# A decoder layer on one core: 128 attention weights a query instead of 256, the farthest keys in pass 1 and pass 3, two buffers for pass 3's loads

## The chip, the cores and the metric

One Trainium2 core of one chip. The metric is device time in microseconds of one execution of the kernel; "before" is the median of 3 runs.

## What is computed

One layer for 2048 tokens of width 1024, in float32. The part that the change touches is the dilated attention: 8 heads of 64, three branches whose results are merged by their softmax denominators.

```python
DILATIONS = ((128, 1), (512, 4), (2048, 16))
...
q = _rope(_rmsnorm(q.reshape(B, S, N_HEADS, HEAD_DIM), q_norm[i]), positions)
k = _rope(_rmsnorm(k.reshape(B, S, N_HEADS, HEAD_DIM), k_norm[i]), positions)
...
kk = jnp.concatenate([k_prev, kb], axis=2)
scores = jnp.einsum('nbqhd,nbkhd->nbhqk', qs, kk).astype(jnp.float32) * (HEAD_DIM ** -0.5)
dist = (jnp.arange(BLK)[:, None] + BLK) - jnp.arange(2 * BLK)[None, :]
band = (dist >= 0) & (dist <= n_back)
...
w = jax.nn.softmax(jnp.stack(lses, axis=0), axis=0)
o = jnp.sum(w[..., None] * jnp.stack(outs, axis=0).astype(jnp.float32), axis=0)
```

Within a residue class a query at place p of its block of 128 sees the keys p to 127 of the block before and the keys 0 to p of its own: 129 keys, of which only place p counts twice. In the third branch there is no block before. Around the attention stand RMSNorm and one input projection to seven groups of 512 columns (q, k, v, gate_B, u, v_A, gate_A), a gMLP mixer per chunk of 128 tokens, an output projection, and a gated per-layer embedding.

## The kernel before, in words

The work runs in three passes over 16 tiles of 128 tokens. Every float32 product is made of three float32r (or float16) products of a high and a low part, so one projection of a tile to 512 columns is 24 matmuls.

**Pass 1** (functions `prep`, `step`, `post_qk`, `turn_qk`, `post_v`, `post_gb`). `prep(n)` normalises tile n of x (L213, L150, L151, L219), turns it with two DMA transposes of 16-bit words (`turn_words`: L182 on ACT, L184 on SP, L186 on DVE) and splits it to `aT` (L196 on ACT, L197 on DVE). `step(n, g)` projects a tile to q, k, v or gate_B. What follows a q or k projection is norm and rotary on DVE and POOL (L411 to L429), a DMA transpose (L438), for k a copy on ACT (L444), and a store to DRAM. The scheduler of the framework sets each engine's order. At the end TensorE's order is written by hand: q of tiles 14 and 15 back to back, then both k, both v, both gates, then the first gMLP chunk, whose weights are loaded by `load_group` (L130 to L138) into the slots of q, k and v as these come free.

**Pass 2** (class `Step`, function `gmlp`). Every head pair and branch has 16 query tiles, in quads of four. A step makes the scores of one tile whose keys are two blocks wide (27 of a head pair's 48 tiles, 108 in all), or of two tiles with one block (first blocks, and all of the third branch): 152 steps. `scores` (L780) fills a PSUM bank, DVE adds the mask and takes the row minimum (L783, L789), ACT makes the weights (L791) in `pr`. `turn`, one step later (LAG_B), splits the 512 weights per query row into two float16 parts (L798 on ACT, L117 on POOL) and turns them by one DMA transpose (L801) from `raw` into `pt`. `values`, six steps after the scores (LAG_C), multiplies with v (L812). Between `turn` and `values` `fill(1.3)` puts 1.3 us of gMLP matmuls (L651, yields of two matmuls for 0.43 us) into TensorE's order.

**Pass 3** (`mixed`, `merge`, `turn_mixed`, `out_proj`, `norm3`, `gate`). `mixed(n)` loads the three branches (`ob`, L602, L604), gate and gMLP output (`ma`, `mg`), `merge` weighs and adds them (L573 to L590). `out_proj` and `gate` are 108 matmuls a tile (L230). Between the passes the last three gMLP chunks run beside the loads of the output weights.

Of the kernel before, what the change touches and what calls it, by code (L numbers as in the profile page):

```python
# [10 lines left out]
F32 = mybir.dt.float32  # L11
F32R = mybir.dt.float32r
F16 = mybir.dt.float16
I32 = mybir.dt.int32
U16 = mybir.dt.uint16
# [21 lines left out]
def _shape_constants():  # L37

    p = np.arange(128)

    def mask(keys, back=False):
        keep = keys[None, :] >= p[:, None] if back else keys[None, :] <= p[:, None]
        return np.where(keep, 0, NEG).astype(np.float32)
    k0 = p.reshape(32, 4).T.reshape(128)
    return {"c_ident": np.eye(128, dtype=np.float32),
            "c_mask": np.concatenate([mask(k0, True), mask(k0), mask(p, True), mask(p)], 1),
            "c_freq": INV_FREQ.reshape(1, 32)}
# [3 lines left out]
PR, PH, OB, SV = 3, 6, 5, 5  # L51

LAG_B, LAG_C = 1, 6

BLOCK0, FILL = 18, 1.3
# [26 lines left out]
def hybrid_layer(ctx: ExitStack, tc: tile.TileContext, io, out):  # L82
# [17 lines left out]
    d_gb = dram.tile([S, 512], F32, name="d_gb")  # L100
    d_at = dram.tile([NT, 128, D], F32, name="d_at")
# [5 lines left out]
    cst.tile([128, 8], F32, name="pad")  # L107
    bs = cst.tile([128, 4], F32, name="bs")
# [151 lines left out]

    def load_qk(qk, hp, c):
# [13 lines left out]
    with ExitStack() as s1, ExitStack() as s1q:  # L275
# [90 lines left out]
        def v_scale():  # L366
# [3 lines left out]
            ones = p1.tile([128, 128], F32, name="ones")  # L370
# [37 lines left out]
        def post_qk(n, which, ps):  # L408
# [8 lines left out]
            m1 = p1.tile([128, HEADS, 2, 32], F32, name="m1", bufs=2)  # L417
# [8 lines left out]
            nc.vector.tensor_tensor(r, r, rs[:, :, None].to_broadcast([128, HEADS, 64]), op=OP.mult)  # L426
            hl = p1.tile([128, HEADS, 2, 64], F16, name="hl", bufs=2)
# [26 lines left out]

        def post_v(n, ps):
# [4 lines left out]
            hi = nc.scalar.activation(vt[:, :, 0, 0:64], z, AF.Copy, scale=sv)  # L460
            lo = nc.vector.scalar_tensor_tensor(vt[:, :, 1, 0:64], z, sv, vt[:, :, 0, 0:64],
# [15 lines left out]
        def gm_constants():  # L477
            for name, src in (("mask", io["c_mask"]), ("wsT", d_ws),
                              ("lng", bcast(io["ln_v_g"], 512)), ("lnb", bcast(io["ln_v_b"], 512))):
                CG[name] = pg.tile([128, 512], F32, name=name)  # L480
                nc.sync.dma_start(CG[name], src)

        def spatial_weights():
# [4 lines left out]
            nc.sync.dma_start(keep[:, 0:128], io["c_mask"][:, 384:512])  # L488
# [11 lines left out]
        def step(n, g):  # L500
# [3 lines left out]
            if g in "qk":  # L504
# [3 lines left out]
                turn_qk(n, which, hl)  # L508
            else:
# [59 lines left out]
    def merge(ob, mx):  # L569
        ov = ob.rearrange("p (b q) e -> p b q e", b=3)  # L570
        nm, den = ov[:, :, :, 130:132], ov[:, :, :, 64:130:65]
        mn = small.tile([128, 4, 2], F32, name="mn")
        nc.vector.tensor_reduce(mn, nm.rearrange("p b q h -> p q h b"), axis=AX.X, op=OP.min)  # L573
        w = small.tile([128, 3, 4, 2], F32, name="w", bufs=3)
        nc.vector.tensor_tensor(w, mn[:, None].to_broadcast([128, 3, 4, 2]), nm, op=OP.subtract)
        nc.scalar.activation(w, w, AF.Exp)
        wd = small.tile([128, 3, 4, 2], F32, name="wd", bufs=3)
        nc.vector.tensor_tensor(wd, w, den, op=OP.mult)
# [3 lines left out]
        nc.vector.tensor_tensor(w, w, mn[:, None].to_broadcast([128, 3, 4, 2]), op=OP.mult)  # L582
        nums = ob[:, :, 0:130].rearrange("p b (h d) -> p b h d", h=2)[:, :, :, 0:64]
        wb = w.rearrange("p b q h -> p (b q) h")[:, :, :, None].to_broadcast([128, 12, 2, 64])
        nc.vector.tensor_tensor(nums, nums, wb, op=OP.mult)  # L585
        o = nums[:, 0:4]
        nc.gpsimd.tensor_tensor(o, o, nums[:, 4:8], op=OP.add)  # L587
        nc.gpsimd.tensor_tensor(o, o, nums[:, 8:12], op=OP.add)
        m = mx.rearrange("p (q h d) -> p q h d", q=4, h=2)
# [6 lines left out]
    def mixed(n):  # L596

        rows = slice(n * 128, (n + 1) * 128)
        ob = pm.tile([128, 12 * OW + 16], F32, name="ob")[:, 0:12 * OW].rearrange("p (b e) -> p b e", b=12)
# [29 lines left out]
    with s2:  # L629
        p2 = s2.enter_context(tc.tile_pool(name="p2", bufs=1))  # L630

        lng, lnb, mask = (CG[n] for n in ("lng", "lnb", "mask"))
# [102 lines left out]
        def first(br, j):  # L735
            return j < (1, 4, NT)[br]
# [19 lines left out]

        class Step:
# [220 lines left out]
```

## Time and profile before

| | |
|---|---|
| runs | 1285.12, 1286.45, 1288.18 us (median 1286.45) |
| profiled execution | 1282.93 us, span 1281.2 us, mean granted clock 0.978 |
| busy in the span | PE 1196.0 us (93%), PEld 973.7, DVE 884.9, ACT 648.3, POOL 513.3 |
| pass 1 | 0 to 416 us, to the end of the second long TensorE idle |
| pass 2 | 416 to 817 us, to the last product with v |
| pass 3 and its start | 817 to 1281 us |

PE is TensorE's matmuls, PEld its weight loads, which overlap them; SPq is SyncE's queue, which issues the DMAs. Times in the trace count from the span's start. The profiled execution is 3.5 us under the median of the runs.

### The profile page before, as it was taken

Reading aid. Unit: us, or ns where it says so; the run is one execution under the profiler, and the core shown is the slowest. Engines: PE = TensorE matmul, PEld = TensorE weight load, DVE = VectorE, ACT = ScalarE, POOL = GpSimd, SP = SyncE. Lnnn points to the kernel's source line nnn. Section 1 sums busy time; section 2 is a strip of 40 time slices with the busy share of each in tenths; the row PEclk is TensorE's granted clock in tenths of the full one; section 3 lists DMA queues with packets and bytes.
Section 4 is the critical chain, followed back from the end, with each engine's and each line's share of the span. In section 5 each row is a group of like instructions: output and inputs, shape, how many; then the busy total and the mean of one; then the engine's idle time right before and its main releaser. Section 6 shows DMA issues by size and latency. Waiting matters only on the chain.

```text
span 1281.2 us, 21314 instructions
## 1 busy us (share of the span) xinstructions
PE 1196.0 (93%) x7166; PEld 973.7 (76%) x7166; DVE 884.9 (69%) x2253; ACT 648.3 (51%) x1273; POOL 513.3 (40%) x454
## 2 busy tenths in 40 slices
PE   5899999999596999999899899969999999999998
PEld 4778888888485787777677688758778888888887
DVE  6885556565576688878777778588766766766733
ACT  5754433433345487677687678333334334334422
POOL 4763334343354465566565556332221121221200
PEclk9999999999898999999999999989999999999999
DMA  7499777768669999999999999845546646655431
GB/s 266 142 220 219 157 171 175 171 173 186 149 182 245 237 194 236 226 223 241 225 222 251 237 193 220 233 148 174 154 120 144 183 122 137 163 147 135 138 91 50
DMA packets 440542, 233.80 MB, mean 182 GB/s; under 512 B 337136, under 2 KB 389104, under 8 KB 440432
## 3 DMA queue, kind: packets, MB, share of 16 engines
q1 hardware_dynamic: 440432, 232.44, 76.2%
q8 instruction: 56, 0.92, 0.3%
q14 instruction: 54, 0.44, 0.1%
HBM read 102.99 MB, written 57.54 MB: 125 GB/s over the span
## 4 chain that ended last, share of the span: by engine, by line
PE 53%; DMA 15%; DVE 14%; issue 7%; ACT 6%; POOL 3%; SPq 2%; DVEq 0%; ACTq 0%; POOLq 0%
PE mm L230 21%; PE gt L230 7%; PE s L230 7%; PE mm L651 7%; DMA pt<-raw 6%; PE pt L230 4%; PE av L230 2%; PE s L780 2%; PE pt L812 2%; DVE pr L783 2%; DMA raw<-w_in 1%; DVE aT L197 1%; DVE wslot L138 1%; DMA st<-hl 1%; DMA ob<-d_o 1%
## 5 line engine op out<-in xcount | busy, mean ns | idle before, releaser
L230 PE MATMUL mm<-wslot,aT 128*128 128x512 f32 x1536 | 365.8, 393 | 20.2 <-ACT aT L196 16.2
L230 PEld LDWEIGHTS mm<-wslot,aT 128*128 128x128 f32 x1536 | 290.9, 190 | 83.9 <-ACT aT L196 18.0
L651 PE MATMUL mm<-wslot,aT 128*128 128x512 f32 x1152 | 314.1, 413 | 24.0 <-DVE gv L642 18.5
L651 PEld LDWEIGHTS mm<-wslot,aT 128*128 128x128 f32 x1152 | 211.2, 195 | 64.1 <-DVE gv L642 19.3
L117 POOL TENSOR_TENSOR raw<-pr,raw 128x512 f16<-128x512 f32 (+1 forms) x152 | 177.8, 1175 | 138.6 <-ACT raw L798 124.2
L791 ACT ACTIVATE pr<-pr,ost 128x256 f32<-128x256 f32 (+1 forms) x384 | 150.1, 451 | 69.5 <-DVE ost L789 64.4
L230 PE MATMUL gt<-wslot,aT 128*128 128x512 f32 x600 | 143.8, 392 | 1.0 <-ACT wslot L136 1.0
L230 PEld LDWEIGHTS gt<-wslot,aT 128*128 128x128 f32 x600 | 112.8, 189 | 25.7 <-ACT wslot L136 2.2
L812 PEld LDWEIGHTS <-pt 128*128 128x128 f16 x1800 | 64.7, 98 | 62.3 <-DMA pt<-raw 33.5
L798 ACT ACTIVATE raw<-pr 128x512 f16<-128x512 f32 (+1 forms) x152 | 93.2, 620 | 33.1 <-DMA pt<-raw 30.6
L812 PE MATMUL pt<-sv,pt 128*128 128x65 f16 x1800 | 81.6, 194 | 21.1 <-DMA pt<-raw 19.0
L783 DVE CUSTOM_DVE_ANT_0 pr<-s,mask 128x256 f32<-128x256 f32 (+1 forms) x256 | 81.1, 357 | 18.3 <-POOL raw L117 14.2
L230 PE MATMUL s<-wslot,aT 128*128 128x512 f32 x384 | 91.1, 392 | 0.0
L424 POOL TENSOR_TENSOR m<-m,m 128x512 f32<-128x512 f32 x32 | 49.8, 1557 | 96.7 <-DVE rsh L150 90.3
L230 PEld LDWEIGHTS s<-wslot,aT 128*128 128x128 f32 x384 | 72.8, 190 | 15.2
L230 PE MATMUL pt<-wslot,aT 128*128 128x512 f32 x336 | 78.3, 389 | 0.0
L230 PEld LDWEIGHTS pt<-wslot,aT 128*128 128x128 f32 x336 | 63.1, 188 | 13.1
L780 PEld LDWEIGHTS <-sq 128*128 128x128 f16 x768 | 69.9, 120 | 3.4 <-issue 1.6
L590 POOL TENSOR_TENSOR ma<-ob,ma 128x512 f32<-128x512 f32 x16 | 24.1, 1506 | 120.0 <-DMA ma<-d_gb 61.1
L780 PE MATMUL s<-sk,sq 128*128 128x256 f16 (+1 forms) x512 | 71.9, 276 | 0.0
L587 POOL TENSOR_TENSOR ob<-ob 128x512 f32<-128x512 f32 x16 | 20.9, 1309 | 124.8 <-DVE ob L585 124.8
L789 DVE TENSOR_SCALAR ost<-ost 128x2 f32<-128x2 f32 (+1 forms) x152 | 63.0, 416 | 2.6
(198 smaller groups left out, 1797.4 us busy)
## 6 DMA issues: line engine op xcount, KB each, us to landing
xt<-x SPq DMA_DIRECT2D x32, 512.0 KB, 4.5
d_o<-ost SPq DMA_DIRECT2D x48, 264.0 KB, 3.7
raw<-w_in SPq DMA_DIRECT2D x38, 256.0 KB, 3.3
sv<-d_vt SPq DMA_DIRECT2D x32, 264.0 KB, 3.7
ob<-d_o SPq DMA_DIRECT2D x16, 528.0 KB, 4.5
xt<-d_at SPq DMA_DIRECT2D x16, 512.0 KB, 4.7
sk<-d_k SPq DMA_DIRECT2D x32, 256.0 KB, 4.6
out<-th SPq DMA_DIRECT2D x32, 256.0 KB, 2.8
```

Source lines behind the costliest of these rows:

```text
L117: nc.gpsimd.tensor_tensor(dst, a, b, op=op)
L230: nc.tensor.matmul(ps, aT[:, ha, k, :], w(slot, hw, k), start=(n == 0), stop=(n == 3 * nk - 1))
L424: add = nc.gpsimd.tensor_tensor(f1, f1, f2, op=OP.add)
L587: nc.gpsimd.tensor_tensor(o, o, nums[:, 4:8], op=OP.add)
L590: nc.gpsimd.tensor_tensor(m, o, m, op=OP.mult)
L651: nc.tensor.matmul(ps, GT[c][:, ha, k, :], slots[g][:, hw, k, :], start=(n == 0), stop=(n == 23))
L780: nc.tensor.matmul(ps[:, c:c + nk], cols(br, j, Q[h]), cols(br, j, K, n, h, self.nb), start=(n == 0), stop=(n == 1))
L783: nc.vector.tensor_tensor_reduce(pr[:, c:c + nk], ps[:, c:c + nk], mask[:, m - nk:m], -1.0, 3e38, op0=OP.add, op1=OP.min, accum_out=o[:, j ...
L789: nc.vector.tensor_scalar(nm, nm, math.log(PSCALE), None, op0=OP.add)
L791: nc.scalar.activation(pr[:, c:c + nk], pr[:, c:c + nk], AF.Exp, bias=o[:, j - j0, 130 + h:131 + h], scale=-1.0)
L798: nc.scalar.activation(ph, pr[:, :width], AF.Copy)
L812: nc.tensor.matmul(PO[0][:, j % 2, h], self.pt[:, t, c // 128], vt[:, h, vv, 0:65], start=(n == 0), stop=(n == 3 * self.nb - 1))
```

## The change

**Pass 2.** For a tile with two key blocks the scores of the own block are overwritten, where the key stands after the query, by those of the block before (`copy_predicated` with the mask as predicate). So 128 weights a query stand for 128 of the 129 keys. A step is now always one tile (192 steps); a `Pair` of tiles 2i and 2i+1 shares one `turn` (96 in all). After the transpose `part` takes the two blocks apart again: DVE ands the words with a table of bits into `pc` (own block), POOL subtracts that from `pt` (block before). The weights' matmuls stay as they were. LAG_C is 9 steps, `part` runs 6 steps after the scores, `fill` takes 0.9 us after a one-block tile and 1.13 us after a two-block tile.

**The 129th key** (one or four tiles back, branches 1 and 2). Pass 1 makes its score by `far_scores` on POOL (product) and DVE (sum), 27 of each, and stores it with plain float32 v (`vr`). Pass 3 loads both and merges them as two more branches.

**Pass 3's loads** `ob`, `ma`, `mg` get two buffers. **Pass 1's tail**: tile 14 is prepared before the steps of tile 13, tile 15 between them.

```diff
-        for g in "qkvg":
+        prep(NT - 2)
+        for g in "qk":
             step(NT - 3, g)
-        prep(NT - 2)
         prep(NT - 1)
+        for g in "vg":
+            step(NT - 3, g)
...
+        def far_scores(n):
+            far = small.tile([128, 2, HEADS], F32, name="far", bufs=2)
+            if n < FAR[1]:
+                nc.vector.memset(far, -NEG)
+            for x, back in enumerate(FAR):
+                if n >= back:
+                    t = p1.tile([128, HEADS, 64], F32, name="m2", bufs=2)
+                    f = t.rearrange("p h d -> p (h d)")
+                    pool_tt(f, RT["k", n - back], RT["q"][1], OP.mult)
+                    nc.vector.tensor_reduce(far[:, x], t, axis=AX.X, op=OP.add, negate=True)
+            nc.sync.dma_start(d_far[n], far)
...
+            nc.scalar.activation(vr, ps, AF.Copy, scale=sv)
+            nc.sync.dma_start(d_vr[n * 128:(n + 1) * 128], vr)
...
+            def part(self, br, after):
+                with tc.issue_after(after.ins):
+                    nc.vector.tensor_tensor(d, a, bits[:, None, None, m:m + 64].to_broadcast([128, 2, 2 * n, 64]),
+                                            op=OP.bitwise_and)
+                pool_tt(a, a, d, OP.subtract)
...
+                if nb == 2:
+                    own = ps[:, :, 128:256]
+                    nc.vector.copy_predicated(own, m.bitcast(U32)[:, None].to_broadcast([128, 2, 128]),
+                                              ps[:, :, 0:128])
+                    self.last = nc.vector.tensor_reduce(top, own, axis=AX.X, op=OP.max, negate=True)
...
+                nc.scalar.activation(top, top, AF.Copy, bias=math.log(PSCALE))
+                for h in range(2):
+                    nc.scalar.activation(pr[:, h], own[:, h], AF.Exp, bias=top[:, h:h + 1],
+                                         scale=1.0 if nb == 2 else -1.0)
...
-LAG_B, LAG_C = 1, 6
+LAG_B, LAG_P, LAG_C = 1, 6, 9
-BLOCK0, FILL = 18, 1.3
+BLOCK0, FILL = 18, (0.9, 1.13)
```

In `merge` two columns of weights, a copy, a product `vr * w` (DVE) and two additions (POOL) are added per tile.

ACT in pass 1, one tile's period, before (`hl<-st` is L444, the copy that waits for the transpose of k; `raw<-xt` starts the next tile's transposes):

```order
L470 ACTIVATE gb<-pt 128x512
L213 ACTIVATE aT,ss<-xt 128x1024
L444 ACTIVATE hl<-st 128x1024
L182 ACTIVATE raw<-xt 128x1024 x2
L411 ACTIVATE sq<-mm 128x512
L182 ACTIVATE raw<-raw 128x256 x4
```

and in the change:

```order
L500 ACTIVATE gb<-pt 128x512
L221 ACTIVATE aT,ss<-xt 128x1024
L440 ACTIVATE hl<-kr 128x8x64
L190 ACTIVATE raw<-xt 128x1024 x2
L456 ACTIVATE hl<-st 128x1024
L421 ACTIVATE sq<-mm 128x512
L190 ACTIVATE raw<-raw 128x256 x4
```

The copy `hl<-st` now stands behind `raw<-xt`, and the rounding of k (`hl<-kr`) ahead of it.

POOL in the same period, in the change (L125 are the two products of the 129th key, L434 the rotary additions, L159 the inverse roots; before, L402, L424, L404, L151 followed each other there):

```order
L159 TENSOR_TENSOR rs<-rs,mhalf 128x1
L434 TENSOR_TENSOR m_2229<-m_2229,m_2230 128x512
L159 TENSOR_TENSOR rsh<-rsh,mhalf 128x8
L412 TENSOR_TENSOR ta<-gA,cs 128x128
L125 TENSOR_TENSOR m_2242<-kr,m_2229 128x512
L125 TENSOR_TENSOR m_2245<-kr,m_2229 128x512
L159 TENSOR_TENSOR rsh<-rsh,mhalf 128x8
L434 TENSOR_TENSOR kr<-kr,m_2282 128x512
L414 TENSOR_TENSOR tb<-gB,sn 128x128
```

Both products stand between the rotary addition of q and that of k.

DVE in pass 2, two-block tiles of the second branch, in the change (L870 folds the blocks, L872 is the row maximum, L838 takes a pair apart, L897 moves the product with v):

```order
L870 COPY_PREDICATED s<-mask,s 128x2x128
L872 TENSOR_REDUCE ost<-s 128x2
L838 TENSOR_TENSOR pc<-pt,bits 128x512
L870 COPY_PREDICATED s<-mask,s 128x2x128
L872 TENSOR_REDUCE ost<-s 128x2
L897 COPY ost<-pt 128x2x130
L870 COPY_PREDICATED av<-mask,av 128x2x128
L872 TENSOR_REDUCE ost<-av 128x2
```

Where two tiles had four L783 with their read-outs and two L789, they now have two foldings, two maxima, and one L838 that waits for a transpose in this queue.

## Rows read from the trace of the kernel before

**Rows 1.** The page's chain that ended last, share of the span by engine.

```profile
PE 53%; DMA 15%; DVE 14%; issue 7%; ACT 6%; POOL 3%; SPq 2%; DVEq 0%; ACTq 0%; POOLq 0%
```

**Rows 2.** Busy us by engine in stretches of 50 us; then clock, DMA share, GB/s.

```profile
100.00:150.00 50.00, 50.00 (x222) 41.44 (x221) 28.18 (x56) 20.61 (x35) 19.37 (x18) 1.00 0.84 198
...
850.00:900.00 50.00, 45.40 (x201) 37.02 (x202) 45.04 (x77) 21.48 (x39) 15.35 (x12) 0.93 0.52 166
...
1000.00:1050.00 50.00, 50.00 (x222) 41.39 (x221) 34.83 (x70) 20.06 (x37) 9.62 (x8) 1.00 0.58 161
```

**Rows 3.** TensorE's waits in 350:400, 400:450 and 450:800: us, times, longest.

```profile
PE mm L230 <- ACT aT L196: 13.8, 1, 13.8
...
PE mm L651 <- DVE gv L642: 12.3, 1, 12.3
...
PE pt L812 <- DMA pt<-raw: 15.7, 19, 2.5
```

**Rows 4.** Timeline of TensorE, behind the two long waits of pass 1.

```profile
352.57 8.01 PE L230 MATMUL mm<-wslot,aT 128*128 128x512 f32 x24 [13.75 <-ACT aT L196]
...
416.41 8.49 PE L651 MATMUL mm<-wslot,aT 128*128 128x512 f32 x24 [12.32 <-DVE gv L642]
```

**Rows 5.** Timeline of DVE: the last split of tile 5 and of tile 15.

```profile
119.70 0.69 DVE L197 TENSOR_TENSOR aT<-raw,aT 128x512 fp32r<-128x512 f32 x1
...
355.61 0.68 DVE L197 TENSOR_TENSOR aT<-raw,aT 128x512 fp32r<-128x512 f32 x1
```

**Rows 6.** Timeline of ACT: the copy of k ahead of the next tile's words.

```profile
342.83 1.13 ACT L444 ACTIVATE hl<-st 128x1024 f16<-128x1024 f16 x1 [3.31 <-DMA st<-hl]
```

**Rows 7.** Timeline: an addition on POOL and the small operation of DVE beside it.

```profile
355.84 1.59 POOL L424 TENSOR_TENSOR m<-m,m 128x512 f32<-128x512 f32 x1 [0.49 <-DVE m L421]
356.21 1.24 DVE L150 TENSOR_SCALAR rsh<-ssh 128x8 f32<-128x8 f32 x1
```

**Rows 8.** Groups of instructions, shapes apart: busy us, mean ns, idle before.

```profile
L117 POOL TENSOR_TENSOR gv<-gv,lng 128x512 f32<-128x512 f32 x16 | 20.6, 1289 | 9.5 <-DVE gv L669 6.4 <-ACT raw L798 0.9 <-DVE ost L789 0.8
L428 ACT ACTIVATE hl<-m 128x512 f16<-128x512 f32 x32 | 20.2, 630 | 79.6 <-DVE m L426 79.6
L413 DVE TENSOR_REDUCE ssh<-sq 128x8 f32<-128x512 f32 x32 | 21.8, 680 | 43.4 <-ACT sq L411 43.4
L150 DVE TENSOR_SCALAR rs<-ss 128x1 f32<-128x1 f32 x32 | 4.8, 150 | 12.1 <-ACT aT L213 12.1
```

**Rows 9.** Stretches of pass 2, columns as in rows 2, and their sum.

```profile
417.00:450.00 33.00, 31.09 (x190) 23.87 (x189) 21.15 (x72) 16.51 (x35) 16.40 (x15) 0.92 0.95 230
450.00:480.00 30.00, 30.00 (x297) 24.85 (x296) 25.73 (x116) 24.64 (x58) 19.55 (x19) 1.00 0.94 198
...
sum 400.00, PE 378.77 PEld 304.34 DVE 310.66 ACT 279.20 POOL 237.82; mean PE 29.14 PEld 23.41 DVE 23.90 ACT 21.48 POOL 18.29
```

**Rows 10.** DMA in 450:800: queue's packets, MB, share; issues, median us to landing.

```profile
q1 hardware_dynamic: 173641, 78.21, 107.8%
...
pt<-raw SPq DMA_TRANSPOSE x141, 4.2
```

**Rows 11.** Timeline of TensorE in pass 2: a filling and the values behind it.

```profile
457.26 1.64 PE L651 MATMUL mm<-wslot,aT 128*128 128x512 f32 x6
458.74 0.54 PE L812 MATMUL pt<-sv,pt 128*128 128x65 f16 x12
```

**Rows 12.** Groups on DVE: a two-block tile of pass 2, and a 256-element operation on PSUM.

```profile
L421 DVE TENSOR_TENSOR m<-s,tb 128x256 f32<-128x256 f32 x32 | 11.9, 413 | 0.0
L783 DVE CUSTOM_DVE_ANT_0 pr<-s,mask 128x256 f32<-128x256 f32 x144 | 55.2, 416 | 13.7 <-POOL raw L117 13.2 <-PE s L780 0.2
L789 DVE TENSOR_SCALAR ost<-ost 128x2 f32<-128x2 f32 x112 | 49.0, 438 | 1.8
```

**Rows 13.** Pass 3: the merge on DVE (group), and its wait for `ob` (timeline).

```profile
L585 DVE TENSOR_TENSOR ob<-ob,w 128x1536 f32<-128x1536 f32 x16 | 28.1, 1758 | 1.3
...
1023.43 0.18 DVE L573 TENSOR_REDUCE mn<-ob 128x8 f32<-128x24 f32 x1 [1.54 <-DMA ob<-d_o]
```

More of the change, by code (lines that the diff above doesn't have):

```diff
@@ L107, in hybrid_layer @@
     cst.tile([128, 8], F32, name="pad")
+    small.tile([128, 96], F32, name="pad", bufs=1)
     bs = cst.tile([128, 4], F32, name="bs")
@@ L588, in merge @@
         nc.gpsimd.tensor_tensor(o, o, nums[:, 8:12], op=OP.add)
+        for x in range(nx):
+            nc.gpsimd.tensor_tensor(o, o, t[:, 4 * x:4 * x + 4], op=OP.add)
         m = mx.rearrange("p (q h d) -> p q h d", q=4, h=2)
@@ L790, in scores @@
[L790 to L802 removed]
+                br, nb, o, j, j0 = self.br, self.nb, self.o, self.j, self.j0
@@ L809, in values @@
+                if i == 0:
+                    PO[0] = bank("pt", (128, 2, 2, 65))
+                for h in range(2):
                     n = 0
-                    for vt in self.v[j]:
+                    for w, v in zip((self.pair.pc, self.pair.pt) if self.nb == 2 else (self.pair.pt,), self.v):
                         for t, vv in ((0, 0), (0, 1), (1, 0)):
-                            nc.tensor.matmul(PO[0][:, j % 2, h], self.pt[:, t, c // 128], vt[:, h, vv, 0:65],
+                            nc.tensor.matmul(PO[0][:, i, h], w[:, t, i, h], v[:, h, vv, 0:65],
@@ L823, in hybrid_layer @@
         quads = [(hp, br, j0) for hp in range(4) for br in (0, 2, 1) for j0 in range(0, NT, 4)]
-        plan = [(q, j) for q in quads for j in range(q[2], q[2] + 4, 2 if first(q[1], q[2] + 3) else 1)]
+        plan = [(q, j) for q in quads for j in range(q[2], q[2] + 4)]
         clock = [0.0, 0.0]
@@ L863, in hybrid_layer @@
                         o = p2.tile([128, 4, OW], F32, name="ost", bufs=OB)
-                    steps.append(Step(br, hp, j0, range(j, j + (2 if first(br, j0 + 3) else 1)), qk, o))
+                    if j % 2 == 0:
+                        pair = Pair()
+                    steps.append(Step(br, hp, j0, j, qk, o, pair))
                     steps[n].scores()
                 if 0 <= n - LAG_B < len(plan):
-                    steps[n - LAG_B].turn()
-                    fill(FILL)
+                    s = steps[n - LAG_B]
+                    if s.i:
+                        s.pair.turn()
+                    fill(FILL[s.nb - 1])
+                if 0 <= n - LAG_P < len(plan) and steps[n - LAG_P].i:
+                    steps[n - LAG_P].pair.part(steps[n - LAG_P].br, steps[min(n, len(plan) - 1)].last)
                 if 0 <= n - LAG_C:
```

164 lines of the change are left out of this document (97 added, 67 removed).

## The prediction

> **What bounds the kernel now.** I read the chain that ended last first: 53% of the span is TensorE, 15% DMA, 14% DVE [rows 1]. The mean hides three kinds of stage, so next come the stretches. In 100 to 150 us and in 1000 to 1050 us TensorE is busy all 50 us of 50, with 222 matmuls, 0.225 us each [rows 2]: there only fewer matmuls would help, and the change removes none (768 for scores and 1800 for values stand before and after). What can be won lies between. TensorE's waits show it [rows 3]: one of 13.8 us and one of 12.3 us at pass 1's end, and 19 of together 15.7 us in pass 2, all on the turned weights. Behind a long wait the clock is also lower: 24 matmuls take 8.01 and 8.49 us [rows 4] instead of 24 x 0.225 = 5.4, so the two cost 2.6 and 3.1 us more.
>
> The first wait has a history. Tile 5 is split at 120.4 us, tile 15 at 356.3 [rows 5]: one round of preparing a tile takes 235.9 / 10 = 23.6 us, while TensorE uses up a tile in 96 x 0.225 = 21.6. The lead shrinks with each tile, and where q of tiles 14 and 15 stand back to back it is gone. In that round ACT waits 3.31 us for the transpose of k and copies 1.13 us [rows 6] before it may start the next tile's words.
>
> **The change part by part.**
>
> *Pass 1's round.* In the new order on ACT the wait and the copy stand behind the words: -4.4 us. Ahead of the words comes the rounding of k, 0.63 us [rows 8]. On POOL two products of 128x512 stand ahead of k's addition, priced as the float32 product of 1.29 us [rows 8]: 2.6 us. The sums on DVE (0.68 each, as the sum over the same shape [rows 8]) and the copy of v (about 0.63) have other work to lie beside: DVE is busy 28 of 50 us there, ACT 21 [rows 2]. So a round is 23.6 - 4.4 + 0.6 + 2.6 = 22.4 us. It cannot fall below TensorE's 21.6; with nothing removed and all that is added on the round (2.6 + 1.4 + 0.6) it is 28.2. I take 22.4 since it goes by the rows of the very instructions. Tile 15 is then ready at 120.4 + 224 = 344.4 us, 11.9 earlier, which leaves some 2 us of the first wait.
>
> *Pass 1's end.* From tile 15's split to the product that ends the second wait at 416.4 [rows 4] pass 60.1 us, in which DVE, ACT and POOL finish the last tiles and split 24 pieces of gMLP weights. This work is late next: it now also holds four products on POOL (5.2 us), four sums on DVE (2.7) and two copies (1.3). I put POOL's 5.2 on the path; the ends are 0 and 9.2. SP gets two stores more a tile, and the second half of the words' transposes stands behind the store of k in its queue; the ACT copy it waits for has the first half's transpose beside it, so I cost it at nothing (1.1 us a round if that cover fails). Together pass 2 starts 11.9 - 5.2 = 6.7, say **7 us, earlier**. By the ends of both terms this is 20 us earlier to 55 later.
>
> *Pass 2, room.* From 417 to 817 us TensorE's matmuls are busy 378.8 of 400 us, so idle 21.2. The weight loads tell more: in the stretch from 450 to 480, where no matmul waits, they are busy 24.85 of 30 (82.8%), in all of pass 2 304.3 of 400 [rows 9]. At 82.8% that work fits into 367.4 us, a room of 32.6; less the 3.1 us of slow clock behind the second wait, which stays, 29.5. I take the second reading, because the ends of matmuls in the trace are modelled and a late start hides in them. The Trainium skill (Trainium Kernel Development and Optimization, Performance Expectations) says that matmul busy time is a bad metric, because matmuls are pipelined, and that the busy share of LDWEIGHTS is a good one; by this rule the room is 29.5 and the time 1264 as below, by matmul time 21.2 - 3.1 = 18.1 and 1276. The trace agrees so far as the two readings differ; no row decides between them.
>
> *Pass 2, what the change does to it.* The DMA queue holds 107.8% of 16 engines' time in 450 to 800, with 141 transposes [rows 10]; each moves 128 x 1024 halves, 0.26 MB, so 37 of the 78 MB. A pair of two-block tiles now takes one transpose, not two: 152 become 96, 37% fewer, and by bytes the share falls to about 107.8 x (1 - 0.47 x 0.37) = 89%. The waits for `pt` lose their reason. Against it:
> - TensorE changes over more often: 196 fillings of gMLP matmuls instead of 158. Six take 458.74 - 457.26 = 1.48 us [rows 11] instead of 1.35, so a change costs 0.13; 38 x 0.13 = **4.9 us**.
> - A new wait. L838 on DVE waits for the transpose, then POOL subtracts (0.68 and 1.29 us by the same shapes [rows 8]), then the values may start; behind L838 stand the next tiles' foldings. At about 2 us a step the values come 16 us after the pair's last scores; folding, weights, split, 4.2 us to landing [rows 10], L838 and subtraction come to some 13. That gives no wait on average, and some when POOL or DVE is held by the gMLP. The ends are 0 and the 15.7 us that the waits for the transposes cost now [rows 3]. I take the middle, **8 us**.
> - DVE: a two-block tile took 2 x 0.416 + 0.438 = 1.27 us. Folding and maximum go over 256 elements each, so between 0.41 [rows 12] and 0.68, and L838 adds 0.34 a tile: 1.17 to 1.70. Over 108 tiles that is -11 to +46 us of 310.7 busy in 400 [rows 9]. It is hidden by the 89 us that DVE idles; without that cover it shows as a late L838, in the range above. ACT makes as many exponentials as before, 192 tiny additions more and 56 splits fewer; it idles 121 us.
>
> So pass 2 gains 29.5 - 4.9 - 8 = 16.6, say **17 us**; the ends are 25 and -5 (only the changes-over).
>
> *Pass 3.* In 850 to 900 us DVE is busy 45 of 50 [rows 2]. A merge grows by a product over 1024 elements (two thirds of the 1.76 us for 1536 [rows 13], 1.2) and six small ones of 0.15 to 0.2 [rows 8, 13]: 2.2 us. Three merges in that stretch make 6.6 if all shows. The second buffer takes away waits such as the 1.54 us for `ob` [rows 13], 4.6 for three. I take **2 us later**; the ends are -5 and +11 (five merges, no wait saved). Later, from 1000 to 1050 us, TensorE is busy all the time and DVE 34.8 of 50 [rows 2]; 2.2 us on DVE and 2.6 on POOL per 24 us lie beside it and cost nothing. If DVE's 15 us of slack were used up, `norm3` would come late, by the same 2 us a tile at most.
>
> *Sum:* -7 - 17 + 2 = **-22 us**, against the profiled execution's 1282.9 us 1260.9. The median of the runs is 3.5 us above that execution, so I forecast **1264 us**. A measurement of this kernel can tell about 0.2%, 2.6 us, from no change.
>
> **The rivals.**
>
> *Slower: the products on POOL lengthen pass 1's round.* POOL and DVE hold each other up: an operation of DVE on 8 numbers took 1.24 us beside POOL's addition [rows 7], its like elsewhere 0.15 [rows 8]. Each of the 27 added products of 1.29 us can do that to the round's DVE operations. Half-way to the 28.2 us, at 25.9, tile 15 comes 23 us later, and with 5 us at the end and -15 behind it the time is 1286.5 + 13 = 1300; at 28.2 it is 1322. It decides from a round of 24.6 us. The Trainium skill (SBUF — State Buffer, SBUF: two separate sides) calls the port pair of DVE and GpSimd an exclusive lock, held for a whole instruction; by it each product could block a two-input operation of DVE for its full length, which is this rival. The rows of this case show it for one small operation only. Against it: the 4.4 us that leave the round. Chance 0.13.
>
> *Pass 2 keeps most of its time.* TensorE's work is the same, only 108 of 192 tiles have their weights halved, and L838 with the subtraction may take the full 15.7 us. Then pass 2 gains 29.5 - 4.9 - 15.7 = 9 and the sum is -14: 1272; with no gain there -5: 1281. Chance 0.17, 0.05 of it within 0.2%.
>
> *More than forecast.* The round falls to TensorE's 21.6 us and no new wait comes: -20 - 25 and pass 3 at 0, 1241; half-way from the forecast 1253. For it speaks that the tile loads are then never late. Chance 0.15, priced at 1248.
>
> **How the numbers follow.** The forecast, 1254 to 1274, has 0.55. Faster: 0.55 + 0.15 + 0.12 = 0.82; same 0.05; slower 0.13. The range is 1242 to 1288: it leaves out some 0.06 below and 0.11 above.
>
> **What would show it.** In the changed profile: 96 transposes of `pt` and a DMA share under 95% in pass 2; the first wait of pass 1 under 5 us with a round near 22.4 us between splits; the second wait still there, some 10 us; TensorE's idle in pass 2 under 12 us; no wait of TensorE from the second tile of pass 3 on. The forecast is wrong if the round is over 24.6 us, or if DVE stands at L838 for more than 15 us in all while TensorE's values wait for `pc` or `pt`.

## The result, and the profile after

The changed kernel takes **1305.13 us** (median of 4, 1301.0 to 1307.73) against 1285.85 for the kernel before, run beside it: a ratio of **1.0149** (95% interval 1.0126 to 1.0173), so 1.5% slower. The forecast was 1264, with a range of 1242 to 1288. The profiled execution took 1304.83 us, its span is 1303.1.

Marks on the two timelines show where the time went:

| mark | before | after | stage longer by | forecast |
|---|---|---|---|---|
| first gMLP product behind pass 1's second long wait | 416.4 | 411.6 | -4.8 | -7 |
| end of the last values of pass 2 | 817.0 | 798.8 | -13.4 | -17 |
| out_proj's second addition, tile 2 (index from 0) | 933.8 | 930.6 | +15.0 | +2 |
| the same, tile 11 | 1151.6 | 1177.4 | +29.0 | 0 |
| end of the span | 1281.2 | 1303.1 | -3.8 | 0 |

Passes 1 and 2 gained 18.2 of the 24 us forecast. Pass 3 and the way into it gave back 40. From here on **the round** of pass 3 is the time from out_proj's second addition of tile 5 to that of tile 11 on DVE, divided by six: 24.4 us before, 27.5 after.

The chain that ended last, on the page of the changed kernel; it answers to [rows 1]:

```profile
PE 50%; DVE 16%; DMA 14%; POOL 7%; issue 6%; SPq 4%; ACT 3%; DVEq 0%; POOLq 0%; ACTq 0%
```

The stretches of [rows 2], same columns:

```profile
100.00:150.00 50.00, 50.00 (x222) 41.41 (x221) 31.66 (x60) 22.44 (x38) 22.19 (x22) 1.00 0.91 225
850.00:900.00 50.00, 38.24 (x156) 28.94 (x156) 49.23 (x93) 19.96 (x37) 22.34 (x16) 0.93 0.54 172
1000.00:1050.00 50.00, 45.41 (x191) 36.44 (x189) 30.70 (x63) 16.21 (x29) 15.70 (x12) 0.97 0.52 145
```

In 1000 to 1050 us TensorE made 222 matmuls before and now 191, at a granted clock of 0.97 instead of 1.00, while DVE is *less* busy than it was (30.7 against 34.8) and none of the other engines reaches two thirds. So something waits; and in 850 to 900 DVE is full. What DVE waits for in 1000 to 1200 us tells more. Before, four lines of this view (us in total, times, longest):

```profile
DVE mn L573 <- DMA ob<-d_o: 11.9, 9, 2.1
DVE xt L626 <- PE gt L230: 11.2, 7, 2.2
...
DVE xn L217 <- POOL rs L151: 5.3, 8, 0.7
DVE tm L186 <- DMA ma<-tm: 4.8, 7, 1.2
```

After, its first three:

```profile
DVE xn L225 <- POOL rs L159: 20.9, 7, 3.0
DVE tm L194 <- DMA ma<-tm: 18.7, 7, 4.0
DVE mn L613 <- DMA ob<-d_o: 14.5, 7, 2.9
```

The normalisation of the tile (`xn`) waits 3.0 us each time for its power on POOL (`rs`), which took 0.7 before. The wait for `ob`, which the second buffer was to take away, has grown, and so has that for the words of `ma`. The wait for out_proj's matmuls (`xt` on PE, 11.2 us before) is gone: DVE now comes after TensorE. POOL's timeline shows why `rs` is late: it stands behind the four additions of the merge.

```profile
1010.75 2.20 POOL L636 TENSOR_TENSOR ob<-ob 128x512 f32<-128x512 f32 x1 [10.16 <-DVE ob L629]
1013.03 1.47 POOL L637 TENSOR_TENSOR ob<-ob 128x512 f32<-128x512 f32 x1
1014.58 2.71 POOL L639 TENSOR_TENSOR ob<-ob,vr 128x512 f32<-128x512 f32 x2
1017.25 0.55 POOL L159 TENSOR_TENSOR rs<-rs,mhalf 128x1 f32<-128x1 f32 x1
```

The chain of waits through one round (start, us, what) closes on itself with no TensorE in it:

```profile
1006.32 0.20 DVE mn L613
...
1010.59 1.22 DVE vr L634
1011.81 1.21 DVE xt L681 x2
1013.03 1.47 POOL ob L637
...
1014.58 1.36 POOL ob L639
...
1016.01 1.29 POOL ob L639
1017.32 0.32 SPq L662
...
1018.97 2.42 DMA ma<-tm
...
1023.72 3.12 DMA ma<-d_gb
...
1027.30 1.49 POOL ma L641
1028.81 0.38 SPq L653
...
1029.23 4.55 DMA ob<-d_o
...
1033.88 0.20 DVE mn L613
```

Merge on DVE, out_proj's addition behind it, POOL's additions, a load of `vr` that waits for them on SP, the transposes of `ma` behind that load, the load of the next `ma`, POOL's product, the load of the next `ob`, the next merge: 1033.88 - 1006.32 = 27.56 us. I call this the ring. Every piece stands in some queue behind the one ahead of it, which need not be its data.

### The profile page after: what moved, and what is told of

Read it like the earlier page. It is cut to its first block, busy times and chain, and to the rows that moved or that the text cites. A ratio compares the mean times of both kernels' runs of the same rounds, so it can differ in the third digit from the quotient of the medians.

```text
span 1303.1 us, 21398 instructions
## 1 busy us (share of the span) xinstructions
PE 1204.1 (92%) x7166; PEld 969.7 (74%) x7166; DVE 921.4 (71%) x2051; ACT 640.9 (49%) x1425; POOL 605.6 (46%) x508
## 4 chain that ended last, share of the span: by engine, by line
PE 50%; DVE 16%; DMA 14%; POOL 7%; issue 6%; SPq 4%; ACT 3%; DVEq 0%; POOLq 0%; ACTq 0%
PE mm L706 14%; PE mm L238 10%; PE s L238 5%; DMA ob<-d_o 5%; PE pt L893 4%; PE pt L238 4%; PE gt L238 4%; PE s L865 4%; PE av L238 2%; POOL ob L639 2%; PE av L865 2%; DMA ma<-d_gb 2%; DMA ma<-tm 1%; SPq L192 1%; DVE wslot L146 1%
## 5 line engine op out<-in xcount | busy, mean ns | idle before, releaser
L238 PE MATMUL mm<-wslot,aT 128*128 128x512 f32 x1536 | 376.1, 400 | 44.2 <-ACT aT L204 29.3
L706 PE MATMUL mm<-wslot,aT 128*128 128x512 f32 x1152 | 319.8, 413 | 20.4 <-DVE gv L697 15.7
L125 POOL TENSOR_TENSOR raw<-pr,raw 128x512 f16<-128x512 f32 x96 | 115.0, 1198 | 61.3 <-ACT raw L822 46.2
L636 POOL TENSOR_TENSOR ob<-ob 128x512 f32<-128x512 f32 x16 | 35.1, 2193 | 136.8 <-DVE ob L629 136.8
L125 POOL TENSOR_TENSOR pt<-pt,pc 128x512 int32<-128x512 int32 (+1 forms) x56 | 70.5, 1259 | 54.9 <-issue 18.2
L238 PEld LDWEIGHTS s<-wslot,aT 128*128 128x128 f32 x384 | 72.0, 188 | 16.8 <-POOL wslot L146 1.9
L893 PE MATMUL pt<-sv,pt 128*128 128x65 f16 x1152 | 77.1, 194 | 7.9 <-POOL pt L125 7.9
L880 ACT ACTIVATE ost<-ost 128x2 f32<-128x2 f32 x192 | 38.1, 199 | 82.5 <-DVE ost L872 53.1
L893 PEld LDWEIGHTS <-pt 128*128 128x128 f16 x1152 | 54.5, 97 | 30.5 <-issue 21.5
L221 ACT ACTIVATE aT<-xt 128x1024 fp32r<-128x1024 f32 x32 | 34.0, 1063 | 68.7 <-DVE xt L681 66.2
L159 POOL TENSOR_TENSOR rs<-rs,mhalf 128x1 f32<-128x1 f32 x32 | 20.6, 643 | 96.8 <-DVE rs L158 96.8
L897 DVE COPY ost<-pt 128x260 f32<-128x260 f32 x96 | 40.7, 424 | 31.0 <-PE pt L893 30.5
```

The costliest lines, as they stand in the source:

```text
L125: nc.gpsimd.tensor_tensor(dst, a, b, op=op)
L159: nc.gpsimd.tensor_tensor(dst, dst, mhalf[:, :width], op=OP.pow)
L221: nc.scalar.activation(aT[:, 0].rearrange("p k t -> p (k t)"), xt, AF.Square, accum_out=ss)
L238: nc.tensor.matmul(ps, aT[:, ha, k, :], w(slot, hw, k), start=(n == 0), stop=(n == 3 * nk - 1))
L706: nc.tensor.matmul(ps, GT[c][:, ha, k, :], slots[g][:, hw, k, :], start=(n == 0), stop=(n == 23))
L880: nc.scalar.activation(top, top, AF.Copy, bias=math.log(PSCALE))
```

## Experiments

All are compared with the kernel before, run on the same chip beside them (its medians lie between 1281.9 and 1284.4 us). 18 kernels ran; a ratio stands where a kernel was executed several times, and the others have one execution and no interval. The round comes from one profiled execution of each kernel; that of power_first_one was the fastest of ten (1274.9 us, median 1280.8), so its 26.0 may be a little low.

| run | us | ratio to before (95%) | round |
|---|---|---|---|
| no_far_merge | 1270.6 | 0.9912 (0.9885 to 0.9939) | 24.1 |
| one_buffer | 1302.1 | 1.0155 (1.0123 to 1.0188) | 27.2 |
| two_vr | 1303.1 | 1.0162 (1.0135 to 1.0189) | 27.1 |
| no_far_add | 1291.2 | one execution | 25.1 |
| idle_products | 1304.4 | one execution | 27.2 |
| merge_behind_norm | 1327.0 | 1.0336 (1.0298 to 1.0373) | 30.6 |
| late_merge | 1321.6 | 1.0312 (1.0276 to 1.0349) | 29.5 |
| late_merge_pool_queue | 1308.2 | 1.0214 (1.0188 to 1.024) | 28.6 |
| far_product_behind_norm | 1385.8 | one execution | 33.5 |
| vr_on_pool_queue | 1292.7 | 1.0084 (1.0053 to 1.0114) | 27.5 |
| power_first_one | 1280.8 | 0.999 (0.9967 to 1.0013) | 26.0 |
| vr_on_pool_queue_two | 1310.0 | 1.0217 (1.0189 to 1.0244) | 27.4 |
| power_first_two | 1298.4 | 1.0134 (1.0085 to 1.0184) | 25.8 |
| product_behind_norm | 1271.3 | 0.9903 (0.9882 to 0.9924) | 25.5 |
| product_behind_norm_old_tail | 1271.2 | 0.9901 (0.9881 to 0.9922) | 25.7 |
| old_tail | 1304.1 | 1.0163 (1.0133 to 1.0192) | 27.2 |
| merge_behind_norm_old_tail | 1326.2 | 1.0343 (1.0298 to 1.0388) | 30.5 |
| no_products | 1316.7 | one execution | 27.5 |

### The far parts, or the buffers?

**no_far_merge**: the merge of before in the changed kernel.

```diff
-        merge(ob, mx[0], n, vr)
+        merge(ob, mx[0])
```

> The changed kernel with the merge of before: pass 3 loads and merges no far key, so the output lacks the share of the key 128 (and 512) back; pass 1 and pass 2 as changed, two buffers kept. Ring theory: the round is TensorE's 24.2 us again, 29 us less over nine rounds, and the transition gets some 10 us shorter: about 1262 to 1270 us, so faster than the kernel before. Buffer theory: the round stays over 26 us and the time over 1290.

**one_buffer**: `bufs=2` taken from ob, ma and mg. **two_vr**: the same, and `bufs=2` for vr.

```diff
-        ob = pm.tile([128, 12 * OW + 16], F32, name="ob", bufs=2)...
-        mx = [pm.tile([128, 512], F32, name=m, bufs=2) for m in ("ma", "mg")]
+        ob = pm.tile([128, 12 * OW + 16], F32, name="ob")...
+        mx = [pm.tile([128, 512], F32, name=m) for m in ("ma", "mg")]
```

> The changed kernel with one buffer again for ob, ma and mg in pass 3. Ring theory (in steady pass 3 the load of ob, the merge on DVE, out_proj's addition behind it, the words of ma on ACT, the transposes, the load of ma, POOL's product and the next load of ob form a ring, which the far parts made longer than TensorE's 24.2 us): the steady round stays at 27.4 us (27 to 28). Buffer theory (the second buffers made the scheduler hoist the merges, and that costs the rounds): the round falls to 24 to 25 us and the time by some 25 us. For the transition both expect that three merges instead of five ahead of the first out_proj leave DVE freer: from the second to the third out_proj 30 to 40 us instead of 50, so some 10 us less in all by the ring theory: about 1293 us.

> As one_buffer (one buffer for ob, ma, mg), but two buffers for vr, so that its loads no longer wait on SP for POOL's additions ahead of the transposes of ma. Ring theory: the 1.7 us that the transposes stood behind that load and the 0.6 us of its second part leave the ring: a round of 25.1 us (24.5 to 25.7), some 20 us less than one_buffer. If the ring is not what sets the round but the load of DVE or POOL is: the round stays within 0.5 us of one_buffer's.

**no_far_add**: POOL's far additions left out.

```diff
-        for x in range(nx):
-            nc.gpsimd.tensor_tensor(o, o, t[:, 4 * x:4 * x + 4], op=OP.add)
```

> The changed kernel without POOL's additions of the far products in the merge (27 of 128x512; the output lacks the far key's share; loads and DVE's products stay). Ring theory: 2.7 us of POOL leave the two ways through the ring (the norm's power behind the additions, and vr's load that waits for them on SP): a round of 24.5 to 25.5 us instead of 27.4. If DVE's longer merge alone makes the ring too long: 26.5 us or more.

Without the far parts in the merge the round is TensorE's again, and the kernel beats the one before by 0.9%. Its stretch, and the whole chain of waits in 1000 to 1060 us:

```profile
1000.00:1050.00 50.00, 50.00 (x222) 41.43 (x221) 33.36 (x63) 22.07 (x39) 9.54 (x8) 1.00 0.59 148
```

```profile
by line: PE mm L238 70.6%; PE gt L238 18.1%; PE s L238 11.3%
```

So all of the loss comes with the far parts of pass 3's merge, and the rest of the change is worth some 13 us (1283.5 - 1270.6).

The buffers do not make the round: 27.2 us with one. They do make the way into pass 3 longer: from the last values to tile 2 it takes 119.5 us with one buffer, 131.8 with two, 116.8 before. With two, four merges stand ahead of the first out_proj addition instead of three, and a fifth follows at once, where DVE has no room (49.2 of 50 us above). Of these 12 us 5 come back behind tile 11, where the merges then run out two tiles earlier, and 3 in the nine rounds before it; the two times agree within their intervals.

two_vr did not test what it was made for: the scheduler used the second buffer to issue vr's load a tile earlier, and SP waited for POOL as before. no_far_add shortens the round by 2.4 us, for 2.7 us of additions.

### The work, or its place?

**merge_behind_norm**: the merge queued behind the norm of two tiles before.

```diff
-            if n + 2 < NT:
-                prep3(n + 2)
+            if n + 3 < NT:
+                with tc.issue_after(XN[0]):
+                    mixed(n + 3)
+            if n + 2 < NT:
+                turn_mixed(n + 2, p3)
```

> The changed kernel, all its work and buffers kept; in pass 3 the merge of tile n + 3 is queued on DVE behind the normalisation of tile n + 1 (and so behind out_proj's addition of that tile), where the second buffer of ob lets its load be under way. Ring theory: the addition no longer stands behind a merge that waits for ob, nor the norm's power on POOL behind the merge's additions; the ring is cut and the round is TensorE's 24.2 us (24 to 24.8) with no wait of TensorE in the middle of pass 3: some 29 us less over nine rounds, about 1265 to 1276 us, faster than the kernel before. Load theory (the added work on DVE and POOL is itself what is too much): the round stays over 26 us, since no work is left out.

**late_merge**: queued behind out_proj's addition of two tiles before; **late_merge_pool_queue**: also vr's loads on POOL.

```diff
-        mixed(n)
+        with tc.issue_after(ADD[n - 2]):
+            mixed(n)
```

> The changed kernel, all its work and both buffers kept; the merge of tile k + 2 is queued on DVE behind out_proj's addition of tile k, instead of that of tile k + 4 ahead of it. The load of ob then has to wait only for a product of the round before. Ring theory: a round of 24.2 to 25.5 us and, with fewer merges ahead of the first out_proj, about 1265 to 1285 us. Load theory: the round stays over 27 us and the time over 1297. If the merge behind the addition makes the norm late instead (it stands ahead of it on DVE), a round of 25.5 to 28 us with TensorE waiting for the turned norm.

> As late_merge, with vr's loads issued by POOL, so that no load of vr stands on SP. Ring theory: 24.2 to 25 us a round, up to 10 us less than late_merge. If SP's queue no longer matters once the merge is late: within 4 us of late_merge.

**far_product_behind_norm**: one_buffer, with two things moved.

```diff
+            with tc.issue_after(XN[0]):
                 nc.vector.tensor_tensor(t, t, wx..., op=OP.mult)
...
+                with tc.issue_after(far_ob.ins):
                     nc.sync.dma_start(vr..., d_vr...)
```

> As one_buffer, with the far product on DVE (1.22 us) queued behind the normalisation of the tile before, and so POOL's far additions behind the norm's power, and vr's loads queued on SP behind those of ob. All work is kept. Ring theory, if the rest of the order stays: a round of 24.2 to 25.5 us, some 1270 to 1285 us. The place of ob's load on SP moves too, ahead of the transposes of ma; if its wait for POOL's product then holds those transposes, the round stays over 27 us by that new way.

**idle_products**: no_far_merge, with work of the same size on a scratch tile.

```diff
+        t = pm.tile([128, D], F32, name="vr").rearrange(...)
+        nc.vector.tensor_tensor(t, nums[:, 0:8], wb[:, 0:8], op=OP.mult)
...
+        for x in range(2):
+            nc.gpsimd.tensor_tensor(t[:, 0:4], t[:, 4:8], t[:, 0:4], op=OP.add)
```

> As no_far_merge, with idle work of the far parts' size in each merge: a product of 1024 elements on DVE into a scratch tile and two additions of 512 on POOL in it; no loads, no small operations; the output lacks the far key. Load theory: the work is what counts, so 26.5 us a round or more. Ring theory: without the loads on SP and with the product put behind the addition by the order, 24.2 to 25.8 us.

Four attempts to cut the ring failed: the same work gave rounds from 28.6 to 33.5 us. In each, a wait moved to another queue. In late_merge and late_merge_pool_queue DVE waits 32.8 and 30.2 us in 1000 to 1200 us for `xt`'s load, which SP issues behind a store of `out`, and SP itself stands at the load of `far`, ahead of the transposes of `ma` and `xn`, until the merge has read the one before (45.5 us in late_merge_pool_queue). late_merge's line:

```profile
SPq L610 <- DVE w L618: 52.3, 7, 8.7
```

In merge_behind_norm it is `xt`'s load too, which waits on SP behind a load of `mg`; the first of DVE's waits in 1000 to 1200 us:

```profile
DVE xt L682 <- DMA xt<-x: 43.6, 7, 7.1
```

In far_product_behind_norm it is the transposes on SP, which stand for the normalisation on DVE; the expectation had named the load of ob ahead of them, and that was not it:

```profile
SPq L192 <- DVE xn L226: 70.1, 6, 12.4
```

These misses say that the order alone moves the round by 6 us with no work added; they do not say which place counts, nor through what. A new order also changes which operations of DVE and POOL run beside each other: in merge_behind_norm, beside POOL's additions, DVE's two copies of `mg`'s words took 2.40 us and the split of `pT` 1.50, against 0.80 and 0.42 in the changed kernel. No run separates the two.

idle_products came out as its load theory had it, and not as its ring theory: without any load of vr, and with nothing but work of the same size, the round is 27.2. The load that I saw in the ring is not what makes it long; when it goes, another way of nearly the same length remains. POOL's timeline there:

```profile
1066.92 1.30 POOL L626 TENSOR_TENSOR ob<-ob 128x512 f32<-128x512 f32 x1 [10.35 <-DVE vr L624]
...
1072.30 0.55 POOL L159 TENSOR_TENSOR rs<-rs,mhalf 128x1 f32<-128x1 f32 x1
```

The norm's power again ends a row of four operations on POOL, and `xn` on DVE waits 2.9 us for it at the longest. That left one suspect.

### One order on POOL

**vr_on_pool_queue** (one buffer) and **vr_on_pool_queue_two** (two) take vr's loads off SP:

```diff
-                nc.sync.dma_start(vr[:, 512 * x:512 * x + 512], d_vr...)
+                nc.gpsimd.dma_start(vr[:, 512 * x:512 * x + 512], d_vr...)
```

> As one_buffer, with vr's loads issued by POOL instead of SP; POOL runs them in order behind the additions that free vr, so that they wait for nothing there and stand ahead of no transpose on SP. In the order that comes of it the norm's power also stands ahead of the merge's additions on POOL. All work is kept. Ring theory: the transposes of ma start as soon as their words are there (2.3 us less in the ring) and the other way through the ring, by the norm's power, gets 2 to 3 us shorter: the round falls from 27.8 to 24.2 to 25.5 us, the time to 1268 to 1285. Load theory: the same work on DVE and POOL, so a round over 27 us and a time over 1297.

> The same move of vr's loads to POOL's queue in the changed kernel itself, with its two buffers. Ring theory: 24.2 to 25.5 us a round, and, with merges hoisted by two tiles, a longer transition than with one buffer but the ring's end two tiles earlier: 1265 to 1283 us. Load theory: over 27 us a round, over 1297.

**power_first_one** and **power_first_two** are these two with the additions queued behind the power (`RN[n]` is the power of tile n's norm; d is 2 with one buffer, 4 with two):

```diff
+        with tc.issue_after(RN[n - d]):
             nc.gpsimd.tensor_tensor(o, o, nums[:, 4:8], op=OP.add)
...
```

> As vr_on_pool_queue (one buffer, vr's loads on POOL), with the merge's additions queued on POOL behind the norm's power of the tile whose addition on DVE stands next; the same work. If the power behind the additions is what sets the round: the wait of the normalisation for POOL falls from 3.0 to 0.7 us, the split of tm is no longer held beside POOL's second addition, and the round falls from 27 to 28.4 us to 24.5 to 25.8; the time from 1292.7 to 1262 to 1280 us. If the sum of the work sets it, round and time stay within 0.5 us and 6 us.

> As vr_on_pool_queue_two, with the same order on POOL. If the power is what sets the round: 24.5 to 25.8 us instead of 27.95, and 1278 to 1292 us instead of 1310. If not: within 6 us of 1310.

Moving the loads alone missed: 27.5 and 27.4 us. (The time still fell by 9.4 us with one buffer, where the way into pass 3 went from 119.5 to 106.6 us, and rose by 4.9 with two.) I had expected the power ahead of the additions in that order; it stayed behind them, and `xn` waited up to 4.6 us. With that one order changed the round falls by 1.4 and 1.6 us and the time by 11.9 and 11.7 us, in both pairs. POOL's timeline of power_first_one:

```profile
1041.45 0.56 POOL L161 TENSOR_TENSOR rs<-rs,mhalf 128x1 f32<-128x1 f32 x1 [13.03 <-DVE rs L160]
1041.98 1.28 POOL L639 TENSOR_TENSOR ob<-ob 128x512 f32<-128x512 f32 x1
1043.34 1.64 POOL L640 TENSOR_TENSOR ob<-ob 128x512 f32<-128x512 f32 x1
1045.06 2.72 POOL L642 TENSOR_TENSOR ob<-ob,vr 128x512 f32<-128x512 f32 x2
```

and DVE's wait for it, in 1000 to 1200 us:

```profile
DVE xn L227 <- POOL rs L161: 5.4, 8, 0.7
```

The expected fall to 24.5 to 25.8 us was reached with two buffers (25.8) and just missed with one (26.0); the times missed, 1280.8 by 1 us and 1298.4 by 6. The load theory in its pure form, by which round and time would have stayed, is out: the work is the same.

The 1.4 us are not all the power's wait. In vr_on_pool_queue the chain of waits runs through TensorE in 1030 to 1075 us, and the first matmuls behind a wait take longer than the next ones; the granted clock is 0.95 in 1000 to 1150 us there and 1.00 in power_first_one. Two pieces of that chain:

```profile
1030.62 8.51 PE mm L238 x24
1039.13 5.44 PE gt L238 x24
```

And the two splits of `tm` on DVE, which lay beside POOL's second addition, take 0.75 us instead of 1.86, while `xn` takes 1.78 instead of 0.75. How much each gives was not separated.

**product_behind_norm** is power_first_one with the far product moved on DVE (`XD[n]`: the normalisation of tile n); **product_behind_norm_old_tail** has pass 1's old tail as well.

```diff
+            with tc.issue_after(XD[n - 2]):
                 nc.vector.tensor_tensor(t, t, wx..., op=OP.mult)
```

> As power_first_one, with the far product on DVE (1.22 us) queued behind the normalisation of the tile two before instead of ahead of out_proj's addition; all work kept, the other orders as they were. If the ring is what is left: 1.2 us less, a round of 24.4 to 25.2 us instead of 26.0, and 1266 to 1276 us instead of 1280.8: faster than the kernel before by 0.5 to 1.2%. If the sum of the work is: 25.7 us or more, 1277 or more.

> As product_behind_norm, with pass 1's tail in the old order: in two pairs so far it started pass 2 some 3 us earlier and changed the time by about 1 us, so 0 to 4 us less than product_behind_norm, 1263 to 1276 us.

All the work is there, and the kernel is **0.97% faster than the one before** (0.9903, 0.9882 to 0.9924). The time came out as expected, the round did not: 25.5, not 24.4 to 25.2. In its new place the far product runs beside POOL's additions and takes nearly twice as long (1000 to 1170 us, the changed kernel, then product_behind_norm):

```profile
L634 DVE TENSOR_TENSOR vr<-vr,w 128x1024 f32<-128x1024 f32 x6 | 7.3, 1218 | 0.0
```

```profile
L638 DVE TENSOR_TENSOR vr<-vr,w 128x1024 f32<-128x1024 f32 x6 | 13.9, 2320 | 0.0
```

TensorE's stretch has one form of wait left; this is all of it from 1000 us to the end:

```profile
PE mm L241 <- ACT aT L206: 2.6, 6, 0.7
```

But in 1000 to 1150 us DVE is now busy 124 us of 150 (101 before), and TensorE makes 646 matmuls instead of 663:

```profile
1000.00:1150.00 150.00, 147.69 (x646) 120.55 (x645) 124.05 (x212) 58.32 (x106) 50.59 (x46) 1.00 0.60 161
```

Where its gain on the changed kernel lies, by the two traces (35 us): 22 us between the last values and tile 5, that is on the way into pass 3 and in the three rounds behind it, and 12 in the six rounds to tile 11. Four edits make it, in this order of runs: one buffer (1.0149 to 1.0155), the loads on POOL (to 1.0084, none of it in the steady round), the power first (to 0.999), the product behind the norm (to 0.9903).

### Pass 1

**old_tail** puts the tail's steps back in their order (q, k, v, g of tile 13, then both preparations); **no_products** leaves the far products out.

```diff
-                    pool_tt(f, RT["k", n - back], RT["q"][1], OP.mult)
-                    nc.vector.tensor_reduce(far[:, x], t, axis=AX.X, op=OP.add, negate=True)
+                    pass
```

> The changed kernel with pass 1's tail in the old order (q, k, v, g of tile 13, then the preparation of tiles 14 and 15). The forecast put all of the 4.4 us a round into the new order of the ACT copy, which is not undone by this; the tail's new order should have brought tile 15 forward: without it the first long wait of pass 1 is 8.8 us plus 2 to 5, and pass 2 starts at 414 to 417 us instead of 411.6; the time is 3 to 5 us longer than the changed kernel's, about 1309. If the tail's order is worth nothing, the start stays at 411 to 412.

> The changed kernel without the far products of pass 1 (27 products on POOL and 27 sums on DVE left out, the table of far scores filled with the constant that makes their weight nothing, so the far key is missing from the output). If the products lengthen pass 1's round as the forecast had it (2.6 us), the round between splits falls from 23.0 to 20.5 to 21.6 us and the first long wait goes; if they lie beside other work it stays at 22.7 to 23.1 us with a wait of 5 to 9 us. Pass 3 keeps its round of 27.4 us.

The tail's new order is worth nothing: 1304.1 against 1305.1 us, and in the other two pairs 1326.2 against 1327.0 and 1271.2 against 1271.3. In old_tail's trace the first long wait is 5.6 us, not longer than 8.8.

no_products surprised: with less work pass 1's round grew from 23.0 to 24.3 us (splits of tiles 5 and 15 at 118.5 and 361.6) and the first wait from 8.8 to 18.5. The reason is the order on ACT. With the products in, the copy of k comes late enough to wait for nothing; without them it stands ahead of the next tile's words again, as before. ACT's copy in 120 to 330 us (busy us, mean ns, idle before), first of the changed kernel, then of no_products:

```profile
L456 ACT ACTIVATE hl<-st 128x1024 f16<-128x1024 f16 x9 | 9.9, 1096 | 0.4 <-DMA st<-hl 0.4
```

```profile
L456 ACT ACTIVATE hl<-st 128x1024 f16<-128x1024 f16 x9 | 10.3, 1142 | 36.0 <-DMA st<-hl 36.0
```

## Why the prediction was wrong

**What held.** *Pass 2.* 96 transposes, a DMA share of 86.4% (89 was forecast), and a new wait for POOL's subtraction of 7.9 us in all (8 taken as the middle). In 450 to 800 us, then TensorE's wait in 430 to 820:

```profile
q1 hardware_dynamic: 123379, 67.54, 86.4%
```

```profile
PE pt L893 <- POOL pt L125: 7.9, 7, 2.1
```

The pass took 387.2 us instead of 400.6, and 1005 instead of 990 gMLP matmuls were done by its end (15 x 0.225 = 3.4 us), so the gain is 13.4 + 3.4 = 16.8 against 17. Here two readings of the room were weighed: by matmul time 5 us would have been left, by the weight loads 17. The Trainium skill (Trainium Kernel Development and Optimization, Performance Expectations) calls matmul busy time a bad metric and the busy share of LDWEIGHTS a good one; the 16.8 us of this trace agree with it. TensorE's idle time in the pass fell by 13.0 us (21.2 to 8.2, under the 12 that were named); the 4.9 us for changing over were not measured by themselves.

*Pass 1's second wait* is still there, 11.5 us where some 10 were named. The first is 8.8 us, not under 5 (340 to 430 us):

```profile
PE mm L706 <- DVE gv L697: 11.5, 1, 11.5
PE mm L238 <- ACT aT L204: 8.8, 1, 8.8
```

**Pass 1's round was mis-sized.** It is (351.2 - 120.9) / 10 = 23.0 us, not 22.4, and tile 15 came 5.1 us earlier, not 11.9. ACT's wait ahead of the copy went, 27.6 us in nine rounds before and 0.4 now, but ACT's next words now wait 26.4 us in these rounds for `xt` on DVE, which they did not before. The copy before, then the words now, 120 to 330 us:

```profile
L444 ACT ACTIVATE hl<-st 128x1024 f16<-128x1024 f16 x9 | 10.0, 1112 | 27.6 <-DMA st<-hl 27.6
```

```profile
L190 ACT ACTIVATE raw<-xt 128x1024 uint16<-128x1024 uint16 x18 | 18.1, 1050 | 26.4 <-DVE xt L227 26.4
```

The two products were priced at 1.29 us and took 1.77, the group in the same stretch:

```profile
L125 POOL TENSOR_TENSOR m<-kr,m 128x512 f32<-128x512 f32 x18 | 31.6, 1772 | 8.8 <-DVE rsh L158 8.8
```

With that price the sum gives -4.4 + 0.6 + 3.5 = -0.3; measured were -0.6. That the two are close does not show that the round is made of these terms. The 5.2 us of POOL that I put on the path behind tile 15 do not lie on it: from its split to the second wait's end it takes 411.6 - 351.2 = 60.4 us, before 60.1. The two errors (6.8 and 4.9 us) cancel for the most part, which is luck.

**The second buffers were booked with the wrong sign.** I took 4.6 us off the way into pass 3, since the load of `ob` would no longer wait. But a buffer only allows; the scheduler used it to move merges ahead, into the stretch where DVE is full. one_buffer's way is 2.7 us longer than before, where the sum without that saving has 6.6; with two it is 15.0.

**The step that failed is the one on steady pass 3.** "2.2 us on DVE and 2.6 on POOL per 24 us lie beside it and cost nothing", with the bound that `norm3` comes late "by the same 2 us a tile at most". The sizes were about right (the far product 1.22 us, POOL's two additions 2.7); the overlap was wrong, and the bound with it. I read the slack of engines (DVE 34.8 of 50) where the slack of the ring was needed. Before, TensorE was the longest way round by a little: in a round DVE waited only some 1.5 us for out_proj's last matmuls, which I passed over. The added product on DVE stands in the ring ahead of out_proj's addition, the added additions on POOL ahead of the power, and the round grew by 3.1 us; over the nine rounds from tile 2 to tile 11 (3.2 each) that makes the 29 us. What shows this: the loss goes with the far parts (no_far_merge), comes back with idle work of their size (idle_products), and two changes of order that keep all work (power_first_one, product_behind_norm) take 2.0 of the 3.1 us off the round again. So the place of the work makes most of the steady loss. For the last 1.1 us, and for how much of the rest is waiting in a queue and how much DVE and POOL holding each other up, the cause stays open.

**The rival that said slower** had a price of 1300 to 1322 us, and 1305 lies in it; but that is luck: its mechanism did not happen. It was to decide at a round of 24.6 us in pass 1, which is 23.0, although the products were held up (1.77 us for 1.29). A rival on pass 3's loop, which is the one that came true, was not among them.

Also open: whether both orders together with the second buffers would do better; that was not tried.

## What to carry to other kernels

Before work is called hidden, follow one round of the loop through every in-order queue back to where it started, and compare that length with the bottleneck's, not the engines' busy shares with 100%: here DVE idled 15 of 50 us, ACT 30 and POOL 40, and the loop had some 1.5 us of slack. Look for the small operation that many wait for (here a power on 128 numbers) and what is queued ahead of it; putting it first was worth 12 us twice, while taking "the" wait out of the chain did nothing for the round, because a second way of the same length stood behind it. A second buffer or less work lets a scheduler choose another order, so read the new order before booking the gain, and see whether operations moved come to lie beside others that hold them up.

## What the runs showed of the hardware

DVE and POOL hold each other up by up to a whole operation, in far more places than the one row that I had. The merge's first addition on POOL takes 2.21 us when DVE's far product follows the near one, and 1.30 without it (the changed kernel and no_far_merge, 1000 to 1170 us):

```profile
L636 POOL TENSOR_TENSOR ob<-ob 128x512 f32<-128x512 f32 x6 | 13.3, 2214 | 59.0 <-DVE ob L629 59.0
```

```profile
L624 POOL TENSOR_TENSOR ob<-ob 128x512 f32<-128x512 f32 x6 | 7.8, 1301 | 52.7 <-DVE ob L622 52.7
```

The other way round, DVE's copies of `ma`'s words take 0.45 us in the changed kernel and 1.38 in product_behind_norm, where POOL's additions run beside them:

```profile
L196 DVE COPY tm<-ma 128x512 uint16<-128x512 uint16 x12 | 15.9, 1378 | 0.0
```

The Trainium skill (SBUF — State Buffer, SBUF: two separate sides) calls the port pair that the two share an exclusive lock for a whole instruction; these rows agree with it. They also explain a wait that the trace puts down to the wrong engine: ACT's words of `ma` start 0.36 us after POOL's second addition ends, though they use nothing of it. What they overwrite is `tm`, and DVE's two splits of `tm` were held beside that addition (1.86 us for both, 0.75 where nothing runs beside them).
